# Five buffers for the gathers, ten for the chunks, later sums of sets, and a register load moved to its branch

## The chip, the cores and the metric

The kernel is one program on one core of a Trainium2 chip. The metric is the device time of one execution in microseconds (us). TensorE is called PE, VectorE DVE, ScalarE ACT, GpSimd POOL and SyncE SP, as in the profile.

## The reference, cut to what matters

Two transformer blocks follow each other on 256 tokens of width 1024 (float32). The first ends in a mixture of experts (32 experts, two for each token). The second ends in a layer that looks up a table of 16384 "keys", and the change is in that layer, apart from one register load in the experts. The layer computes:

```python
# per token: 8 heads, 16 of 16384 entries each, so 128 picked entries
eidx = jnp.take_along_axis(cidx, pos, axis=-1)
g = jax.nn.softmax(best, axis=-1)
a = jnp.einsum('chkd,cd->chk', u_tab[eidx], xc)      # u_tab, v_tab: 16384 x 1024
wgt = (jax.nn.gelu(a) * g)
return jnp.einsum('chk,chkd->cd', wgt, v_tab[eidx])
```

## The kernel before

The key layer treats its 256 tokens in two ways at the same time.

**160 tokens by the whole table (the chunks).** The table is read in 128 chunks of 128 entries. The U loop (128 chunks `ut`, line 1640) multiplies each chunk with the 160 tokens: eight matmuls 128x160 on PE give the products of 128 entries, ACT takes them through the gelu (L1601, L1604) into a tile `B`. From chunk `C0` = 40 on, 40 steps of `gbuild` put the routing weights into `B`, four tokens at a step: DVE and ACT prepare (L1949 to L1955), PE multiplies (L1965), DVE multiplies into `B` (L1968, whose shape holds the number of chunks that are done: 128x104x4 stands beside chunk 104). A step falls due every 2.2 chunks (88 chunks for 40 steps). The V loop (128 chunks `v`, line 1648) then multiplies `B` with the table V, and the eight PSUM banks `acc` collect all 128 chunks. A chunk is 512 KB. Chunks come in through the queue of SP (L87, and L76 for the slices of the tile `xm`), in turn into 14 buffers: four `wA`, three `hi`, three `lo` and four slices of `xm`. A load can start when PE has done with the buffer's chunk of 14 before.

**96 tokens by gathers.** They form three sets of 32 tokens. For a set, 32 gathers (L1765, POOL, an indirect DMA of 128 rows of U and V, 1 MB each) bring the rows that were picked, four entries of each token at a time. For each gather DVE takes the dot products with the tokens (L1793, into `ga`), ACT the gelu of 128 numbers (L1794), DVE multiplies with the weight (L1777) and adds the V half to the set's sum (L1779; L1784 for the first of a set). The sums are called `xa`, `xd0`, `xd1` (`xd` in the profile). When a set is complete, eight small matmuls (L1653, 128x32) add it to `acc`. These read the sum, and PE executes in order.

The order of the gathers is that of a generator, `gathered`: each `next` issues the dot of one gather, the add of the one before and a new fetch. The function `gathers` calls it 9 times in 20 chunks of the U loop and 7 times in 20 chunks of the V loop. A fetch also waits for the matmul of PE that was written last when it was written (`pace_pe`), so it can't run ahead of that place. Before, three fetches are written first, and then one behind each add, two gathers ahead of the dot:

```python
for i in range(3):
    fetch(i)
...
    if i:
        add(i - 1)
        fetch(i + 2)
```

The gathers' tiles `g` come from a pool of three (`gp`), in which some earlier tiles of the layer lie too. A scheduler puts the instructions of each engine into one order ahead of the run; it may move an instruction up or down where the data allow it, and the engine then executes in that order.

The set's sum is put in the V loop behind the first chunk from the third on at which the generator has completed the set:

```python
if c > 1 and ns < len(self.sums):
    for k in range(8):
        summed(ns, k)
    ns += 1
```

In the experts, `many` is the count of the fullest expert. All engines load it into a register (`nc.values_load`), and the branch `tc.If(many > 64)` in `overflow` (L924) reads it. Before, the load is written ahead of the loop over the experts.

Of the kernel before, what the change touches and what calls it, by code (L numbers as in the profile page):

```python
# [8 lines left out]
F32 = mybir.dt.float32  # L9
# [10 lines left out]
D = 1024  # L20
S = 256
# [23 lines left out]
class K:  # L45
# [693 lines left out]
    def moe(self):  # L739
        nc, me, A = self.nc, self.me, self.A  # L740
# [34 lines left out]
        def v(shape, dt=F32):  # L775
            return self.T(me, [128] + shape, dt)
# [56 lines left out]
        cnt, cmax, cmi = v([32]), v([1]), v([1], I32)  # L833
# [1 line left out]
        nc.vector.tensor_reduce(cmax, cnt, axis=AX.X, op=OP.max)  # L835
        nc.vector.tensor_copy(cmi, cmax)
        self.R, self.W, self.cnt, self.cmi, self.xnh, self.xnl = R, W, cnt, cmi, xh, xl
        many = nc.values_load(cmi[0:1, 0:1], min_val=0, max_val=S)
        wg = A["w_gate"].rearrange("e (p k) f -> e p k f", p=128)
        wu = A["w_up"].rearrange("e (p k) f -> e p k f", p=128)  # L840
        wd = A["w_down"].rearrange("e (p j) d -> e p j d", p=128)
# [62 lines left out]
        cur = experts(0, 28)  # L904
        for _ in bg:
            pass

        pools = self.wpools
        self.wi = 0
# [632 lines left out]
    def peer(self):  # L1542
        nc, A = self.nc, self.A
        tt, ts, stt = nc.vector.tensor_tensor, nc.vector.tensor_scalar, nc.vector.scalar_tensor_tensor
        xm = self.xm
# [42 lines left out]
            next(rg)  # L1588
        self.expand(x32)

        w4 = self.T(self.px, [128, 4, 1024], F32, "xm")
        self.wpools = [(self.wA, "wA")] * 4 + [(self.hp, "hi")] * 3 + [(self.hp, "lo")] * 3
        self.wpools += [(None, w4[:, i, :]) for i in range(4)]
        self.wi = 0
        gb = ga = self.pace_pe = None
        tau = 0
# [12 lines left out]
        def gathers(n):  # L1609

            nonlocal ga
            if ga is None:
                if not self.picked:
                    return
                ga = self.gathered()
                self.g0, self.gn = n, 0

            while self.gn < min(nj, (n - self.g0) * 9 // 20 if n < 128 else
                                (128 - self.g0) * 9 // 20 + (n - 128) * 7 // 20):
                next(ga, 0)  # L1620
                self.gn += 1
# [25 lines left out]
        def prod(c, k, w):  # L1647
            self.pace_pe = nc.tensor.matmul(acc[k][:, N0:], w[:, k * 128:(k + 1) * 128], B[:, c, :],  # L1648
                                            start=c == 0, stop=c == 127)

        def summed(s, k):

            nc.tensor.matmul(acc[k][:, s * self.GN:(s + 1) * self.GN], self.sums[s][:, k * 128:(k + 1) * 128], self.sel,  # L1653
                             start=False, stop=False)

        ns = 0
        for c in range(126):
            gathers(128 + c)
            w = self.wload(A["v"][c], [1024])
            for k in range(8):  # L1660
                prod(c, k, w)
            if c > 1 and ns < len(self.sums):
                for k in range(8):
                    summed(ns, k)
                ns += 1
# [89 lines left out]
    def gathered(self):  # L1755

        nc, A = self.nc, self.A
        stt = nc.vector.scalar_tensor_tensor
        J, n = self.GJ, self.NS * self.GJ
        buf, acc = {}, self.T(self.rt, [128, D], F32, "xa")  # L1760

        def fetch(i):
            if i < n:
                buf[i] = self.T(self.gp, [128, 2 * D], F32, "g")
                ins = nc.gpsimd.indirect_dma_start(  # L1765
                    out=buf[i], out_offset=None, in_=A["uv"],
                    in_offset=bass.IndirectOffsetOnAxis(ap=self.gi[:, i // J, i % J:i % J + 1], axis=0))
                if self.pace_pe:

                    self.tc.add_manual_dep(ins.ins, self.pace_pe.ins.name, mybir.DependencyInfo(  # L1770
                        mybir.DependencyClass.Sync, mybir.DependencyReason.DATA), reason="pace")

        def add(i):
            nonlocal acc
            s, j = i // J, i % J
            t, a, w = buf.pop(i)[:, D:], self.ga[:, s, j:j + 1], self.gw[:, s, j:j + 1]
            nc.vector.tensor_tensor(w, w, a, op=OP.mult)  # L1777
            if j:
                stt(acc, t, w, acc, op0=OP.mult, op1=OP.add)  # L1779
            else:  # L1780
                if s:

                    acc = self.gx[s - 1]
                nc.vector.tensor_scalar(acc, t, w, None, op0=OP.mult)  # L1784
            if j == J - 1:
                self.sums.append(acc)

        for i in range(3):
            fetch(i)
        for i in range(n):  # L1790
            s, j = i // J, i % J
            t, a = buf[i][:, 0:D], self.ga[:, s, j:j + 1]
            stt(t, t, 1.0, self.gx[s], op0=OP.mult, op1=OP.mult, accum_out=a)  # L1793
            nc.scalar.activation(a, a, AF.Gelu_apprx_tanh)  # L1794
            if i:
                add(i - 1)
                fetch(i + 2)
            yield
        add(n - 1)

# [354 lines left out]
```

## Time and profile before

| | us |
|---|---|
| median of 3 runs (1623.05 to 1627.79) | 1625.93 |
| the profiled execution | 1625.43 |
| its span in the trace | 1623.6 |
| PE busy in the span | 1527.8 |

The times of the trace count from the start of the span. The profiled execution took 1.8 us more than its span, and it lies 0.5 us under the median. The U loop begins on PE at about 982 us and the V loop at 1304.78 us; the last of its products ends at 1607.9 us, and what follows is the norm of the result and its way out.

### The profile page before, as it was taken

Reading aid. Unit: us, or ns where it says so; the run is one execution under the profiler, and the core shown is the slowest. Engines: PE = TensorE matmul, PEld = TensorE weight load, DVE = VectorE, ACT = ScalarE, POOL = GpSimd, SP = SyncE. Lnnn points to the kernel's source line nnn. Section 1 sums busy time; section 2 is a strip of 40 time slices with the busy share of each in tenths; the row PEclk is TensorE's granted clock in tenths of the full one; section 3 lists DMA queues with packets and bytes.
Section 4 is the critical chain, followed back from the end, with each engine's and each line's share of the span. In section 5 each row is a group of like instructions: output and inputs, shape, how many; then the busy total and the mean of one; then the engine's idle time right before and its main releaser. Section 6 shows DMA issues by size and latency. Waiting matters only on the chain. (4 is left out here: it accounts for less than half of the span.)

```text
span 1623.6 us, 25732 instructions
## 1 busy us (share of the span) xinstructions
PE 1527.8 (94%) x9872; PEld 1200.8 (74%) x9872; DVE 960.9 (59%) x2117; ACT 496.0 (31%) x1222; POOL 120.1 (7%) x122
## 2 busy tenths in 40 slices
PE   7999799999999997979999899999999999699996
PEld 6978644543444443358679699999999999699996
DVE  6986622344535432279888899856667656544443
ACT  4444332232222221155344543235444400000001
POOL 0000000000000000000000100311111112111111
PEclk9999899999999998989999999999999999799998
DMA  9548779999999998965657558999999999999992
GB/s 371 182 132 301 273 277 381 381 418 410 418 419 418 419 418 342 417 223 155 210 185 270 185 169 303 376 404 345 366 363 356 357 409 415 416 413 413 414 414 80
DMA packets 135324, 536.53 MB, mean 330 GB/s; under 512 B 16179, under 2 KB 17180, under 8 KB 122780
## 3 DMA queue, kind: packets, MB, share of 16 engines
q1 hardware_dynamic: 117184, 426.07, 69.1%
q0 software_dynamic: 13824, 100.67, 15.5%
q10 hardware_dynamic: 4188, 8.09, 1.4%
q8 instruction: 79, 1.29, 0.3%
q14 instruction: 49, 0.40, 0.1%
HBM read 532.57 MB, written 2.10 MB: 329 GB/s over the span
## 5 line engine op out<-in xcount | busy, mean ns | idle before, releaser
L1793 DVE SCALAR_TENSOR_TENSOR g<-g,xd 128x1024 f32<-128x1024 f32 x96 | 117.5, 1224 | 140.6 <-DMA g<-in_uv_dram,gi 140.6
L1031 PE MATMUL ps<-wB,XT 128*64 128x512 f32 x492 | 133.2, 609 | 4.7 <-PEq L924 4.6
L1765 POOL DMA_INDIRECT g<-in_uv_dram,gi x96 | 98.8, 1029 | 505.6 <-PE ps L1648 121.1
L132 PE MATMUL ps<-xh,hi 128*128 128x256 f32 x416 | 122.9, 296 | 1.6 <-ACT hi L97 1.6
L1067 DVE SCALAR_TENSOR_TENSOR eyl<-ps,slotw,eyh 64x512 fp32r<-64x512 f32 x64 | 47.6, 743 | 119.0 <-ACT eyh L1066 118.7
L138 PE MATMUL ps<-xh,lo 128*128 128x256 f32 x416 | 117.4, 283 | 0.5 <-DVE lo L98 0.5
L137 PE MATMUL ps<-xl,hi 128*128 128x256 f32 x416 | 117.5, 283 | 0.3 <-DVE xl L305 0.3
L1794 ACT ACTIVATE ga<-ga 128x1 f32<-128x1 f32 x96 | 19.4, 202 | 314.9 <-DVE g L1793 314.9
L1031 PEld LDWEIGHTS ps<-wB,XT 128*64 128x64 f32 x492 | 39.6, 139 | 80.5 <-issue 74.0
L97 ACT ACTIVATE hi<-wA 128x1024 fp32r<-128x1024 f32 x63 | 66.6, 1059 | 76.6 <-PE ps L137 28.8
L98 DVE TENSOR_TENSOR lo<-wA,hi 128x1024 fp32r<-128x1024 f32 x63 | 77.7, 1237 | 20.2 <-ACT hi L97 18.2
L1640 PE MATMUL ps<-x,wA 128*128 128x160 f32 x608 | 87.4, 302 | 0.1
L1648 PE MATMUL ps<-B,wA 128*128 128x160 f32 x608 | 85.9, 300 | 0.0
L1640 PEld LDWEIGHTS ps<-x,wA 128*128 128x128 f32 x608 | 84.9, 193 | 0.3 <-issue 0.3
L132 PEld LDWEIGHTS ps<-xh,hi 128*128 128x128 f32 x416 | 79.3, 191 | 7.7 <-issue 4.4
L1080 DVE TENSOR_TENSOR h<-h,ps 128x512 f32<-128x512 f32 x64 | 42.2, 682 | 70.3 <-PE ps L1078 70.3
L1648 PEld LDWEIGHTS ps<-B,wA 128*128 128x128 f32 x608 | 83.5, 190 | 0.0
L137 PEld LDWEIGHTS ps<-xl,hi 128*128 128x128 f32 x416 | 79.4, 191 | 3.9 <-issue 3.1
L1640 PE MATMUL ps<-x,xm 128*128 128x160 f32 x576 | 81.4, 299 | 0.0
L1648 PE MATMUL ps<-B,xm 128*128 128x160 f32 x576 | 81.2, 302 | 0.0
L1779 DVE SCALAR_TENSOR_TENSOR xd<-g,gw,xd 128x1024 f32<-128x1024 f32 x62 | 79.7, 1285 | 2.1
L1648 PEld LDWEIGHTS ps<-B,xm 128*128 128x128 f32 x576 | 80.1, 193 | 0.0
(531 smaller groups left out, 3364.4 us busy)
## 6 DMA issues: line engine op xcount, KB each, us to landing
wB<-in_w_gate_dram SPq DMA_DIRECT2D x70, 512.0 KB
wB<-in_w_down_dram SPq DMA_DIRECT2D x63, 512.0 KB
wB<-in_w_up_dram SPq DMA_DIRECT2D x53, 512.0 KB
wA<-in_ws_dram SPq DMA_DIRECT2D x51, 512.0 KB
wA<-in_ut_dram SPq DMA_DIRECT2D x38, 512.0 KB
wA<-in_v_dram SPq DMA_DIRECT2D x38, 512.0 KB
wA<-in_w_gate_dram SPq DMA_DIRECT2D x36, 512.0 KB
wA<-in_w_up_dram SPq DMA_DIRECT2D x36, 512.0 KB
```

The lines of the kernel that those rows point to most:

```text
L97: ins = self.nc.scalar.activation(hi, w, AF.Copy)
L98: self.last_split = self.nc.vector.tensor_tensor(lo, w, hi.bitcast(F32), op=OP.subtract)
L132: ins = mm(ps, ah, bh, start=first, stop=False)
L137: mm(ps, ah, bl, start=False, stop=False)
L138: mm(ps, al, bh, start=False, stop=last)
L1031: nc.tensor.matmul(p[64 * s:64 * s + 64, :], XT[:, k, :], w[s][:, a, :], start=k == 0, stop=k == 7)
L1067: nc.vector.scalar_tensor_tensor(y[1][r, s, :], p[r, :], w, y[0][r, s, :].bitcast(F32), op0=OP.mult, op1=OP.subtract)
L1640: self.pace_pe = nc.tensor.matmul(p, w[:, k, :], x32[:, k, N0:], start=k == 0, stop=k == 7)
L1648: self.pace_pe = nc.tensor.matmul(acc[k][:, N0:], w[:, k * 128:(k + 1) * 128], B[:, c, :], start=c == 0, stop=c == 127)
L1765: ins = nc.gpsimd.indirect_dma_start(out=buf[i], out_offset=None, in_=A["uv"], in_offset=bass.IndirectOffsetOnAxis(ap=self.gi[:, i // J, i ...
L1779: stt(acc, t, w, acc, op0=OP.mult, op1=OP.add)
L1793: stt(t, t, 1.0, self.gx[s], op0=OP.mult, op1=OP.mult, accum_out=a)
```

## The change

It gives the gathers two more buffers and takes four from the chunks: the tile `xm` holds two gathers now, so that there are five in all, and the chunks keep `wA`, `hi` and `lo`, ten in all. Five fetches are written first, and then each four gathers ahead of its dot. The sum of a set is written eight chunks later than its completion. The load of `many` is written behind the loop over the first 28 experts.

```diff
-        many = nc.values_load(cmi[0:1, 0:1], min_val=0, max_val=S)
...
         cur = experts(0, 28)
         for _ in bg:
             pass
+        many = nc.values_load(cmi[0:1, 0:1], min_val=0, max_val=S)
...
-        w4 = self.T(self.px, [128, 4, 1024], F32, "xm")
+        self.xg = self.T(self.px, [128, 2, 2 * D], F32, "xm")
         self.wpools = [(self.wA, "wA")] * 4 + [(self.hp, "hi")] * 3 + [(self.hp, "lo")] * 3
-        self.wpools += [(None, w4[:, i, :]) for i in range(4)]
...
-        ns = 0
+        ns, ready = 0, []
...
-            if c > 1 and ns < len(self.sums):
+            if len(ready) < len(self.sums):
+
+                ready.append(max(2, c + 8))
+            if ns < len(ready) and c >= ready[ns]:
                 for k in range(8):
                     summed(ns, k)
                 ns += 1
...
-                buf[i] = self.T(self.gp, [128, 2 * D], F32, "g")
+                buf[i] = self.xg[:, i % 5 - 3, :] if i % 5 > 2 else self.T(self.gp, [128, 2 * D], F32, "g")
...
-        for i in range(3):
+        for i in range(5):
             fetch(i)
...
-                fetch(i + 2)
+                fetch(i + 4)
```

Three places show what the scheduler makes of it. The first is PE in the V loop, at the sum of the second set (`xd_1993`): the last two products of one chunk and the first three of the sum's eight matmuls; the next chunk's products follow those. Before, 36 chunks of the V loop stand ahead of it:

```order
L1648 MATMUL ps_12620<-B_8958,lo_13044 128x160
L1648 MATMUL ps_12621<-B_8958,lo_13044 128x160
L1653 MATMUL ps_12614<-gsel_9975,xd_1993_9694 128x32
L1653 MATMUL ps_12615<-gsel_9975,xd_1993_9694 128x32
L1653 MATMUL ps_12616<-gsel_9975,xd_1993_9694 128x32
```

Now 44 chunks stand ahead of it:

```order
L1647 MATMUL ps_12638<-B_8958,wA_13162 128x160
L1647 MATMUL ps_12639<-B_8958,wA_13162 128x160
L1652 MATMUL ps_12632<-gsel_9975,xd_1993_9694 128x32
L1652 MATMUL ps_12633<-gsel_9975,xd_1993_9694 128x32
L1652 MATMUL ps_12634<-gsel_9975,xd_1993_9694 128x32
```

The eight matmuls moved behind eight more chunks. (The sum of the first set moved from behind 3 chunks to behind 9.)

The second place is DVE in the U loop, where the second set begins: its first add (L1784 before, L1786 now, gather 33 of 96) and the step of `gbuild` beside it. Before, it stands beside chunk 104:

```order
L1793 SCALAR_TENSOR_TENSOR g_11466,ga_9947<-g_11466,xd_1994_9695 128x1024
L1949 TENSOR_TENSOR x_2099_10558<-iotb_8959,lTi_9074 128x1024
L1777 TENSOR_TENSOR gw_9946<-gw_9946,ga_9947 128x1
L1605 TENSOR_TENSOR B_8958<-B_8958,qp_12035 128x116
L1784 TENSOR_SCALAR xd_1993_9694<-g_11466,gw_9946 128x1024
L1605 TENSOR_TENSOR B_8958<-B_8958,qp_12056 128x116
L1968 TENSOR_TENSOR B_8958<-B_8958,ps_12059 128x104x4
```

Now it stands beside chunk 88:

```order
L1795 SCALAR_TENSOR_TENSOR g_11380,ga_9947<-g_11380,xd_1994_9695 128x1024
L1951 TENSOR_TENSOR x_2105_10566<-iotb_8959,lTi_9074 128x1024
L1779 TENSOR_TENSOR gw_9946<-gw_9946,ga_9947 128x1
L1786 TENSOR_SCALAR xd_1993_9694<-g_11380,gw_9946 128x1024
L1604 TENSOR_TENSOR B_8958<-B_8958,qp_11680 128x88
L1604 TENSOR_TENSOR B_8958<-B_8958,qp_11700 128x88
L1970 TENSOR_TENSOR B_8958<-B_8958,ps_11703 128x88x4
```

The gathers' work moved up by 16 chunks here. Over the whole U loop, 42 dots stood ahead of the last step of `gbuild` on DVE, and 51 stand there now; ahead of the first step it was 9 and is 12.

The third place is POOL's queue at the first gathers. Before, they all go to `g`:

```order
L1765 DMA g_10058<-in_uv_dram,gi_9945 128x2048
L1765 DMA g_10060<-in_uv_dram,gi_9945 128x2048
L1765 DMA g_10062<-in_uv_dram,gi_9945 128x2048
L1765 DMA g_10113<-in_uv_dram,gi_9945 128x2048
L1765 DMA g_10163<-in_uv_dram,gi_9945 128x2048
```

Now the fourth and the fifth gather go to `xm`, and the scheduler put them ahead of the third (`g_10064`):

```order
L1767 DMA g_10060<-in_uv_dram,gi_9945 128x2048
L1767 DMA g_10062<-in_uv_dram,gi_9945 128x2048
L1767 DMA xm_9739<-in_uv_dram,gi_9945 128x2048 x2
L1767 DMA g_10064<-in_uv_dram,gi_9945 128x2048
L1767 DMA g_10119<-in_uv_dram,gi_9945 128x2048
```

Two things show nothing to move: the register load (TENSOR_LOAD) stands at the same row as before on each of the five engines, on PE between the last product of the first 28 experts and the branch; and up to the U loop all five engines have the same instructions in the same order. At the very end of PE's order the products of the last two chunks are now interleaved bank by bank, where before all eight of chunk 126 stood ahead of those of chunk 127.

## Rows read from the trace of the kernel before

**Rows 1.** The page: the chain that ended last, share of the span by line.

```profile
PE ps L1640 13%; PE ps L1648 12%; DMA g<-in_uv_dram,gi 5%; PE ps L1965 2%; DVE g L1793 1%; DVE xd L1779 1%; DVE B L1902 0%; DVE lo L98 0%; DMA gi<-g 0%; DMA wA<-in_wq_dram 0%; PE ps L137 0%; PE ps L138 0%; PE ps L132 0%; DVE g L1833 0%; DVE B L1904 0%
```

**Rows 2.** The chain in order of time: start us, us, what.

```profile
1083.20 0.89 PE ps L1965 x8
1084.09 4.35 PE ps L1640 x32
...
1404.29 199.22 PE ps L1648 x1456
```

**Rows 3.** Waits from 1304 to 1401 us: us in total, times, longest.

```profile
POOL g L1765 <- DVE xd L1779: 64.7, 18, 6.2
DVE g L1793 <- DMA g<-in_uv_dram,gi: 29.4, 20, 4.2
...
PE ps L1653 <- DVE xd L1779: 15.7, 1, 15.7
```

**Rows 4.** Timeline of PE: start us, us, [idle before and releaser].

```profile
1311.30 1.87 PE L1653 MATMUL ps<-gsel,xa 128*128 128x32 f32 x16
...
1378.29 6.68 PE L1648 MATMUL ps<-B,lo 128*128 128x160 f32 x48
1400.67 3.62 PE L1653 MATMUL ps<-gsel,xd 128*128 128x32 f32 x16 [15.70 <-DVE xd L1779]
1404.11 8.15 PE L1648 MATMUL ps<-B,xm 128*128 128x160 f32 x48
```

**Rows 5.** Windows: us, busy PE, PEld, DVE, ACT, POOL; granted clock, DMA share, GB/s.

```profile
1086.00:1195.00 109.00, 109.00 (x831) 109.00 (x831) 71.51 (x155) 50.56 (x206) 15.19 (x16) 1.00 0.96 362
...
1385.00:1401.00 16.00, 0.33 (x2) 0.33 (x2) 10.39 (x16) 0.81 (x4) 2.81 (x3) 0.65 1.02 414
...
1421.00:1500.00 79.00, 79.00 (x584) 79.00 (x583) 33.76 (x53) 2.63 (x13) 12.91 (x13) 1.00 1.02 413
```

**Rows 6.** DMA queues from 1304 to 1400 us (q0: gathers, q1: SP).

```profile
q0 software_dynamic: 2979, 21.70, 54.7%
q1 hardware_dynamic: 4946, 18.08, 46.9%
```

**Rows 7.** DMA issues from 1085 to 1304 us.

```profile
g<-in_uv_dram,gi POOLq DMA_INDIRECT x33
```

**Rows 8.** Waits of PE, whole span.

```profile
PE ps L1031 <- PEq L924: 4.6, 1, 4.6
```

**Rows 9.** Timeline of POOL at the first gathers.

```profile
1018.79 1.19 POOL L1765 DMA_INDIRECT g<-in_uv_dram,gi  x1 [38.02 <-DMA gi<-g]
...
1031.29 1.68 POOL L1765 DMA_INDIRECT g<-in_uv_dram,gi  x1 [10.07 <-DVE xa L1784]
...
1048.36 3.39 POOL L1765 DMA_INDIRECT g<-in_uv_dram,gi  x1 [10.36 <-DVE B L1907]
...
1106.61 0.94 POOL L1765 DMA_INDIRECT g<-in_uv_dram,gi  x1 [4.80 <-PE ps L1965]
```

**Rows 10.** Timeline of DVE at the first dots.

```profile
1025.98 1.23 DVE L1793 SCALAR_TENSOR_TENSOR g<-g,xd 128x1024 f32<-128x1024 f32 x1 [4.39 <-DMA g<-in_uv_dram,gi]
...
1040.27 1.23 DVE L1793 SCALAR_TENSOR_TENSOR g<-g,xd 128x1024 f32<-128x1024 f32 x1 [1.18 <-DMA g<-in_uv_dram,gi]
...
1051.70 0.23 DVE L1918 CAST x<-x 128x128 f32<-128x128 bf16 x1
```

**Rows 11.** Timeline of PE at the same place: a chunk, the transposes L1925, a chunk.

```profile
1047.12 2.34 PE L1640 MATMUL ps<-x,wA 128*128 128x160 f32 x16
...
1051.98 0.69 PE L1925 MATMUL ps<-ident,x 128*128 128x128 f32 x2 [2.41 <-DVE x L1918]
1052.46 3.77 PE L1640 MATMUL ps<-x,wA 128*128 128x160 f32 x16
```

**Rows 12.** Timeline at the end: the last product of PE, the last square of ACT.

```profile
1607.48 0.44 PE L1648 MATMUL ps<-B,wA 128*128 128x160 f32 x2
...
1612.18 0.42 ACT L1683 ACTIVATE g<-x 128x256 f32<-128x256 f32 x1
```

## Prediction

> **What bounds the kernel now.** I read the chain that ended last first. In the key layer it runs over the products of the U and V loops on PE, and in one stretch over something else: gathers take 5% of the span and DVE's work on them 2% [rows 1]. PE is busy throughout both loops except for this. The waits from 1304 to 1401 us name it: PE stands 15.70 us before the sum of the second set, because DVE has not finished its adds (L1779); in the same stretch DVE waits for gathers, 29.4 us, and POOL can't issue gathers because DVE has not freed their buffers, 64.7 us [rows 3]. So the second set is late, and its sum stands in PE's order ahead of work that is ready. From 1404.29 us the chain is PE alone for 199 us [rows 2].
>
> Why is it late? A step of `gbuild` falls due every 2.2 chunks, so the U loop takes 2.2 x 2.175 + 0.89 = 5.68 us a step [rows 2]; the generator asks for 9 gathers in 20 chunks, one each 5.74 us. From 1085 to 1304 us, 33 were issued [rows 7], one each 6.64 us: three buffers do not turn round faster when DVE looks at them at its own places. Where the sum stands tells the plan: behind chunk 35 of V, 65 calls, 53 of them in U. Only some 43 were done.
>
> The wait costs more than its length. Granted clock is 0.65 in the window around it [rows 5]: PE, idle, fell to its 1.2 GHz level. The sum took 3.62 us where the first set's took 1.87, and the three chunks behind it 8.15 where the three ahead of it took 6.68 [rows 4].
>
> **The change, part by part.** *The register load* stands at the same row of every engine's order as before: 0. What it could touch is PE's wait at the branch, 4.6 us [rows 8]; a gain of all of it, or as much again lost, are the ends, and neither has an instruction that moved. I take 0 and leave these ends out.
>
> *The sum, eight chunks later,* is due 8 x 2.175 = 17.4 us later [rows 2]; the wait is 15.70 us [rows 4]. This alone covers it, by 1.7 us only. The *five buffers* do more. On DVE 51 dots stand ahead of the last step of `gbuild` in place of 42, so at the V loop's start the gathers are 1 or 2 behind the plan in place of 10, and the second set is complete well ahead of its sum. Gained: 15.70 + (3.62 - 1.87) + (8.15 - 6.68) = **18.9 us** [rows 4].
>
> *What the gathers in U cost.* Nine more dots and adds at about 1.23 us each [rows 10] and small change are 24 us of DVE in some 220 us. DVE is busy 71.51 of 109 us there [rows 5], so 66% becomes 77%: covered by DVE's idle time, on an engine that PE does not wait for there (PE has 109.00 of 109.00). If that cover were gone, each `gbuild` step would be late by up to 0.6 us, 24 us in all; I take 0. The transfers: chunks need 0.524 MB in 5.68/2.2 = 2.58 us, 203 GB/s, gathers now 1.049 MB in 5.74 us, 183 GB/s; sum 386. It moved 362 there, and 413 to 414 where it is kept full [rows 5]. It fits. In V the demand is 241 for chunks (0.524/2.175) and 169 for gathers (7 in 20 chunks), 410 GB/s, as in the stretch from 1421 to 1500 us, where 413 moved and PE did not wait: covered, but with 1% to spare. That the gathers start V ahead, and not behind, is what keeps it so.
>
> *Ten buffers for chunks.* A load is asked for ten chunks ahead, 21.7 us in place of 30.4. Nothing is lost while a load takes less. The danger is a long row of gathers. In the catch-up from 1304 to 1400 us q0 moved 21.70 MB and q1 18.08 [rows 6]: while gathers queue, they come each 4.64 us and chunks get 188 GB/s. Ten chunks less two under way are 4.2 MB in hand. Such a row stands at the beginning. From about 1021 us [rows 9] to chunk 40 at some 1078 us [rows 2] PE needs 241 GB/s, 53 too many, and loses 57 x 0.053 = 3.0 MB. After that it needs 203; the row lasts until DVE's places, 5.7 us apart, have used it up: with 12 dots ahead of the first step and five buffers that is some 25 gathers, 116 us, and another 59 x 0.015 = 0.9 MB. Lost in all: 3.9 MB of 4.2. PE's own waits there (below) give back 1 MB. It holds, narrowly: I take 0; the other end is the second rival.
> The Trainium skill (DMA: Bandwidth & Descriptors, section Queues, rings and completion order) says that each DMA engine serves its queues in turn, packet by packet. By an even split of 414 chunks would get 207 GB/s, and the loss would be 57 x 0.034 = 1.9 MB: 0 with more to spare. The trace splits worse for the chunks, and I go by the trace.
>
> *The first gathers.* Before, DVE waits 4.39 us for gather 0 and 1.18 for another [rows 10], and PE waits 2.41 us at the transposes L1925 for the CAST that DVE issues at 1051.70; the chunk behind it takes 3.77 us, half clock, in place of 2.34 [rows 10, 11]. In DVE's new order five dots stand ahead of this CAST as before, but five adds in place of four; gathers 3 and 4 come right behind 0 and 1, about 4.6 us apart, which makes DVE wait about as long in sum as before. So the CAST comes about one add, 1.2 us, and some tenths later: **+1.5 us** on PE, which stands at the same place of its order. The ends: if all its wait goes, -2.41 - 1.43 = -3.8; if one gather more comes late by its whole spacing, +4.6 + 1.4 = +6. I take the value nearest to the rows of this place.
> POOL took 3.39 us for the issue at 1048.36 us, and 0.94 elsewhere [rows 9]. The Trainium skill (SBUF — State Buffer, section SBUF: two separate sides) says that DVE's two-port operations lock GpSimd out while it writes the descriptors of its own DMAs. By that rule this issue was held 2.45 us, and three gathers issued here would be 7.4 us late, inside DVE's wait for them: the end +6 would become +8.8 with the clock. The trace has one such issue; which operations are two-port ones it does not show.
>
> *The end.* Now each bank's last products stand together, so the first transposes can go out about two products earlier against the last product. ACT's squares end 4.7 us behind that product [rows 12], one of them each 0.54 us, and can begin two earlier: **-1.0 us**, between 0 and -1.2.
>
> The sum: -18.9 + 1.5 - 1.0 = -18.4 us; 1625.43 - 18.4 = 1607.0 for an execution like the profiled one, which lies 0.5 under the median of the three runs. I predict **1607 us**.
>
> **The rivals.**
> 1. *The wait moves to the beginning* (chance 0.08). Dots that now stand earlier in DVE's order than their gathers can land hold up the CAST, and PE at L1925. For it: PE waits there already, and gather 2 had to wait for a buffer 10.07 us [rows 9]. Against: the two `xm` buffers are free then. Time: +6 in place of +1.5, 1611.5.
> 2. *Chunks run dry* (0.15) between 1080 and 1140 us, if the first row of gathers costs 1 MB more than reckoned. PE then waits for single chunks, 1/0.241 = 4.2 us, and half a clock window of 1.4: 1612.6. For it: 0.3 MB in hand by the trace's split. Against: DMA reached only 362 GB/s on average behind this stretch, so what is lost is soon made good.
> 3. *The buffers of `xm` don't work as two* (0.04): the fourth gather holds the fifth, and the gathers begin V still 10 behind. Then chunks get 188 GB/s during the catch-up, 2.79 us each. The ten in hand last 25 chunks, 54 us, in which 54 x (1/4.64 - 1/6.2) = 3 gathers are made up; then PE takes 2.79 us a chunk and asks for a gather each 7.97 us, and the other 7 take 7/(1/4.64 - 1/7.97) = 78 us, 28 chunks at 0.62 us lost: 17 us, 1624, no change.
> 4. *Slower* (0.03): the gathers' queue never empties, and PE gets a chunk each 2.79 us. From 1140 to the V loop that loses 64 x 0.21 = 13 us, in V 0.62 us a chunk up to the last of 96 gathers at 1021 + 445 us, 58 chunks, 36 us: 1656. It decides where the row lasts to the ninth chunk of V. Against it, the pace lets no more than 53 + 4 gathers go in U, 264 us of the 284 up to V.
> 5. *Better than that* (0.02): the wait at L1925 goes, 1602 or less.
>
> The forecast has 0.68, its own range 1603 to 1611. **Numbers.** 0.3% is 4.9 us, about what a measurement of this kernel can tell from no change. Faster than 1621: forecast and rivals 1, 2 and 5, 0.93. Same: rival 3, 0.04. Slower: 0.03. The range from 1602 to 1613 takes in the forecast, rival 1 and most of rival 2; the rest lies beyond.
>
> **What would show it.** Right: no wait of PE for `xd`, the second sum at about 1.9 us, granted clock 1.00 from 1060 us to the end of V, V's 128 chunks and sums in 284 us instead of 303; dots just behind the plan at V's start, the gathers' rate 5.7 us in U, DMA there near 386 GB/s. Wrong: a wait of PE for a chunk's DMA (rivals 2 to 4), a wait longer than 4 us at the transposes (rival 1), or POOL waiting for DVE's adds for most of V (rival 3).

## The result and the profile after

The changed kernel takes 1605.41 us, median of 5 runs (1604.79 to 1606.51); the kernel before, run beside it, 1623.05 (1621.46 to 1627.79). The ratio is 0.9884, 95% interval 0.9867 to 0.9902: by the ratio 18.8 us or 1.2% faster, while the two medians lie 17.6 us apart. Forecast were 1607 us and a range of 1602 to 1613.

The profiled execution took 1605.19 us with a span of 1603.4, against 1625.43 and 1623.6. The starts of the first product of U and of V and the end of the last product of V in the two timelines divide the difference:

| us | before | after | difference |
|---|---|---|---|
| first product of U | 981.8 | 980.4 | -1.4 |
| U, to the first product of V | 323.0 | 324.0 | +1.0 |
| V, to the end of its last product | 303.1 | 284.5 | -18.6 |
| from there to the end of the span | 15.7 | 14.4 | -1.3 |

The first row is no effect of the change: ahead of the U loop all engines have the same order, and over the runs below U begins anywhere between 976 and 983 us. The +1.0 in U is within what executions of one order differ by (load_moved below has the order of before, and 326.4 us). What is left is in V, but for 1.3 us at the end.

PE's timeline of the kernel after, at the sums of the first and of the second set (start us, us, what):

```profile
1324.01 1.87 PE L1652 MATMUL ps<-gsel,xa 128*128 128x32 f32 x16
...
1401.86 1.87 PE L1652 MATMUL ps<-gsel,xd 128*128 128x32 f32 x16
1403.56 4.59 PE L1647 MATMUL ps<-B,wA 128*128 128x160 f32 x32
```

These answer to [rows 4]. Both sums now stand where the plan puts them, neither has an idle time in brackets, and both take 1.87 us; the second took 3.62. The two chunks behind it (32 matmuls) take 4.59 us, where before three (48) took 8.15. The windows say the same of the clock (columns as in [rows 5]):

```profile
1086.00:1195.00 109.00, 109.00 (x830) 108.77 (x829) 80.60 (x171) 51.74 (x209) 20.00 (x19) 1.00 1.02 414
...
1385.00:1401.00 16.00, 16.00 (x120) 16.00 (x119) 7.95 (x12) 0.61 (x3) 2.75 (x3) 1.00 1.03 416
```

In the window that held the wait PE is busy 16.00 of 16 us and the granted clock is 1.00 in place of 0.65. How far ahead the second set now is, DVE's timeline shows at its last add:

```profile
1361.48 1.28 DVE L1781 SCALAR_TENSOR_TENSOR xd<-xm,gw,xd 128x1024 f32<-128x1024 f32 x1
```

It ends at 1362.8 us, 39 us ahead of the sum. The waits from 1304 to 1401 us, to be read against [rows 3]:

```profile
POOL g L1767 <- PE ps L1647: 41.5, 8, 7.0
...
POOL xm L1767 <- PE ps L1647: 29.2, 6, 5.6
...
POOL g L1767 <- DVE xd L1781: 5.6, 1, 5.6
```

POOL waited 64.7 us for DVE's adds there, because the gathers were behind the plan. Now it waits for PE, which is the plan itself: a gather is issued when the chunk that it is tied to has been multiplied. Of the gathers' DMAs, 39 were issued between 1085 and 1304 us in place of the 33 of [rows 7], one each 5.62 us, 16 of them into the two `xm` buffers:

```profile
g<-in_uv_dram,gi POOLq DMA_INDIRECT x23
xm<-in_uv_dram,gi POOLq DMA_INDIRECT x16
```

What is left of PE's waits in U and V stands at the transposes of the second half of the routing (DVE's CAST first, then PE):

```profile
1049.88 0.22 DVE L1920 CAST x<-x 128x128 f32<-128x128 bf16 x1
```

```profile
1050.15 0.69 PE L1927 MATMUL ps<-ident,x 128*128 128x128 f32 x2 [3.62 <-DVE x L1920]
1050.63 4.47 PE L1639 MATMUL ps<-x,lo 128*128 128x160 f32 x16
```

The wait is 3.62 us where [rows 11] show 2.41, and the chunk behind it, at half clock, takes 4.47.

### The profile page after: what moved, and what is told of

The parts are those of the page before. It is cut to its first block, busy times and chain, and to the rows that moved or that the text cites. A ratio compares the mean times of both kernels' runs of the same rounds, so it can differ in the third digit from the quotient of the medians.

```text
span 1603.4 us, 25738 instructions
## 1 busy us (share of the span) xinstructions
PE 1525.1 (95%) x9872; PEld 1199.2 (75%) x9872; DVE 954.9 (60%) x2117; ACT 496.8 (31%) x1222; POOL 125.2 (8%) x122
## 5 line engine op out<-in xcount | busy, mean ns | idle before, releaser
L1795 DVE SCALAR_TENSOR_TENSOR g<-g,xd 128x1024 f32<-128x1024 f32 x58 | 70.9, 1223 | 83.0 <-DMA g<-in_uv_dram,gi 83.0
L1639 PE MATMUL ps<-x,wA 128*128 128x160 f32 x832 | 117.8, 300 | 0.0
L1639 PEld LDWEIGHTS ps<-x,wA 128*128 128x128 f32 x832 | 114.7, 191 | 0.0
L1647 PEld LDWEIGHTS ps<-B,wA 128*128 128x128 f32 x832 | 113.7, 190 | 0.0
L1639 PE MATMUL ps<-x,hi 128*128 128x160 f32 x624 | 88.5, 299 | 0.0
L1767 POOL DMA_INDIRECT g<-in_uv_dram,gi x58 | 65.0, 1121 | 293.7 <-PE ps L1647 115.3
L1647 PE MATMUL ps<-B,hi 128*128 128x160 f32 x608 | 86.6, 300 | 0.0
L1639 PE MATMUL ps<-x,lo 128*128 128x160 f32 x592 | 86.2, 304 | 0.0
L1639 PEld LDWEIGHTS ps<-x,hi 128*128 128x128 f32 x624 | 85.7, 190 | 0.2 <-issue 0.2
L1647 PE MATMUL ps<-B,lo 128*128 128x160 f32 x608 | 84.8, 299 | 0.0
```

Source lines behind the costliest of these rows:

```text
L1639: self.pace_pe = nc.tensor.matmul(p, w[:, k, :], x32[:, k, N0:], start=k == 0, stop=k == 7)
L1767: ins = nc.gpsimd.indirect_dma_start(out=buf[i], out_offset=None, in_=A["uv"], in_offset=bass.IndirectOffsetOnAxis(ap=self.gi[:, i // J, i ...
```

## The experiments

Each ratio is against the kernel before, run on the same chip in the same minutes; that kernel's own median was 1622.7 to 1625.5 us there. The loops' times are from one profiled execution each, taken as in the table above. Such an execution can lie off the median: sum_later's took 1618.29 us, v_eight's 1615.25, spread_six's 1604.73 and spread_mixed's 1598.70.

| kernel | median us | ratio, 95% interval | U us | V us |
|---|---|---|---|---|
| before (first profile) | 1625.93 | | 323.0 | 303.1 |
| after | 1605.41 | 0.9884 (0.9867, 0.9902) | 324.0 | 284.5 |
| sum_later | 1614.12 | 0.9928 (0.9915, 0.9942) | 323.7 | 295.2 |
| buffers_only | 1604.80 | 0.9875 (0.9860, 0.9889) | 324.4 | 284.5 |
| load_moved | 1623.71 | 1.0000 (0.9986, 1.0014) | 326.4 | 303.4 |
| ten_chunks | 1624.75 | 0.9995 (0.9976, 1.0015) | 324.2 | 302.7 |
| four_buffers | 1617.17 | 0.9966 (0.9951, 0.9980) | 320.7 | 297.1 |
| v_eight | 1613.07 | 0.9933 (0.9910, 0.9955) | 324.6 | 291.7 |
| seven_chunks | 1613.90 | 0.9942 (0.9922, 0.9962) | 331.3 | 284.7 |
| cast_first | 1607.88 | 0.9898 (0.9877, 0.9918) | 325.2 | 284.5 |
| spread_six | 1601.49 | 0.9857 (0.9840, 0.9874) | 322.4 | 287.1 |
| spread_seven | 1602.43 | 0.9869 (0.9850, 0.9887) | 323.5 | 284.6 |
| spread_mixed | 1601.16 | 0.9869 (0.9849, 0.9890) | 320.3 | 284.6 |
| after_again | 1606.18 | 0.9888 (0.9868, 0.9908) | 326.9 | 284.5 |

### The parts of the change alone

**sum_later**: the kernel before, with the sums eight chunks later.

```diff
-        ns = 0
+        ns, ready = 0, []
...
-            if c > 1 and ns < len(self.sums):
+            if len(ready) < len(self.sums):
+                ready.append(max(2, c + 8))
+            if ns < len(ready) and c >= ready[ns]:
```

Expected: 

> The kernel before with one part of the change: the sum of a set stands eight chunks later in V; three gather buffers and fourteen for chunks stay. Theory 1 (the place of the sum is what cost the time): the second set is complete at the same 1400.7 us and the sum is due at 1385 + 17.4 = 1402.4, so the 15.70 us and 3.22 us at half clock go and nothing takes their place: 1623.1 - 18.9 = 1604. Theory 2 (mine: late gathers keep a second price, the chunks): in the catch-up chunks get 188 GB/s where PE takes 241, and at V chunk 35 a chunk lands only 4 us ahead of its products. Without the stop PE runs on, the gathers are still about three behind, some 55 us of catch-up are left, and PE waits some 6 us for chunks: 1608 to 1612, with waits of PE for the DMAs of wA, hi, lo or xm between 1390 and 1450 us and none for xd.

Measured: 11.7 us faster (0.0072 of 1625.45), some three fifths of what the change brings. PE's waits from 1380 to 1430 us, and the second sum:

```profile
PE ps L1648 <- DMA wA<-in_v_dram: 2.7, 3, 1.3
PE ps L1648 <- DMA xm<-in_v_dram: 2.7, 4, 1.3
PE ps L1648 <- DMA lo<-in_v_dram: 1.3, 1, 1.3
PE ps L1648 <- DMA hi<-in_v_dram: 0.7, 1, 0.7
```

```profile
1408.32 2.44 PE L1648 MATMUL ps<-B,wA 128*128 128x160 f32 x16 [1.32 <-DMA wA<-in_v_dram]
1410.60 1.64 PE L1653 MATMUL ps<-gsel,xd 128*128 128x32 f32 x14
```

No wait for `xd` is left, and nine waits for chunks, 7.4 us, stand in its place. The gathers are as late as before; as long as they catch up, the DMA queues are full and the chunks come too slowly. So the wait for the sum had a second work, unseen: while PE stood, chunks were loaded. Theory 2 holds, and it had the loss somewhat too small: 1608 to 1612 us were expected, with some 6 us of waits.

**buffers_only**: the kernel after with the sum where it was.

```diff
-            if len(ready) < len(self.sums):
-                ready.append(max(2, c + 8))
-            if ns < len(ready) and c >= ready[ns]:
+            if c > 1 and ns < len(self.sums):
```

Expected: 

> The kernel after with the sum at its old place (behind chunks 2 and 35 of V); five gather buffers, ten for chunks. My theory: with five buffers the second set is complete at 1362.8 us, 22 us ahead of the old place of its sum at 1384.5, so the eight chunks are worth nothing beside the buffers: within 0.3% of 1605.4, no wait of PE for xd. Rival (the sum's place matters by itself, since adds and sums meet at the same time): a wait for xd of several us and 1610 or more.

Measured: 1604.80 us and V in 284.5, the same as with both parts. The second sum, in PE's timeline, and PE's waits in U and V:

```profile
1384.44 1.87 PE L1652 MATMUL ps<-gsel,xd 128*128 128x32 f32 x16
```

```profile
PE ps L1924 <- DVE x L1917: 5.9, 3, 3.9
PE ps L1639 <- DMA hi<-in_ut_dram: 1.1, 1, 1.1
```

The sum stands at its old place and waits for nothing. So the whole gain is the buffers'; beside them the eight chunks are worth nothing that can be measured. The last line is the forecast's second rival, in small: in this execution PE waited 1.1 us for chunk 45 of U.

**load_moved**: the register load at the branch, nothing else.

```diff
-        many = nc.values_load(cmi[0:1, 0:1], min_val=0, max_val=S)
...
         for _ in bg:
             pass
+        many = nc.values_load(cmi[0:1, 0:1], min_val=0, max_val=S)
```

Expected: 

> The kernel before with only the register load written at the branch. My theory: it stands at the same row on every engine, so nothing moves: within 0.3% of 1623.1, the wait at the branch 4.6 us as before. Rival (the load has a part in the gain): 2 to 5 us faster, with a shorter wait at the branch.

Measured: ratio 1.0000, and the waits of before:

```profile
PE ps L1653 <- DVE xd L1779: 13.8, 1, 13.8
PE ps L1925 <- DVE x L1918: 7.6, 2, 5.3
...
PE ps L1031 <- PEq L924: 5.0, 1, 5.0
```

The wait at the branch is there, 5.0 us. The middle line matters for another point: this kernel has the order of before on every engine, and yet its wait at the routing's transposes is 5.3 us where [rows 11] show 2.41. That wait differs by 3 us between executions of one order.

**ten_chunks**: the kernel before with the four `xm` buffers for chunks left unused.

```diff
-        self.wpools += [(None, w4[:, i, :]) for i in range(4)]
```

Expected: 

> The kernel before with ten buffers for chunks in place of fourteen, three for gathers, the sum at its old place. Theory 1 (ten are enough whatever the gathers do): no wait of PE for a chunk, 1623. Theory 2 (mine: ten are enough only where gathers are not behind): a chunk lands some 18 us ahead at V's start in place of 28, the catch-up takes 17 to 24 us of that by V chunk 35, so PE waits some 2 to 6 us for chunks there; but the second sum waits for the same gathers, and its wait of 15.7 us is shorter by as much: 1623 to 1626, with waits for chunk DMAs that the kernel before does not have. Theory 3 (they add up): 1629 or more.

Measured: 0.9995, no change, but PE's waits from 1304 to 1401 us are others than in [rows 3]:

```profile
PE ps L1647 <- DMA lo<-in_v_dram: 3.7, 3, 1.3
PE ps L1647 <- DMA hi<-in_v_dram: 3.1, 3, 1.3
PE ps L1647 <- DMA wA<-in_v_dram: 3.1, 4, 1.2
PE ps L1652 <- DVE xd L1778: 2.4, 1, 2.4
```

9.9 us for chunks and 2.4 for the sum, where it was 15.70 for the sum alone. Theory 2 holds in kind, its size (2 to 6 us) was too small. Both waits hang on the same late gathers, so one shortens by what the other takes.

### What sets the gathers' rate, and how much room the transfers have

**four_buffers**: the kernel after with one `xm` buffer in place of two.

```diff
-                buf[i] = self.xg[:, i % 5 - 3, :] if i % 5 > 2 else self.T(self.gp, [128, 2 * D], F32, "g")
+                buf[i] = self.xg[:, 0, :] if i % 4 == 3 else self.T(self.gp, [128, 2 * D], F32, "g")
...
-        for i in range(5):
+        for i in range(4):
             fetch(i)
...
-                fetch(i + 4)
+                fetch(i + 3)
```

Expected: 

> The kernel after with four gather buffers (one in xm) in place of five; ten for chunks, sums eight chunks later. DVE's order then has 44 dots ahead of the last step of the counting matrix, nearly as few as the 42 before, where five buffers give 51. My theory (the places of dots in DVE's order set the rate in U, not the number of buffers as such): gathers in U come each 6.5 us, they begin V some 7 behind, the catch-up takes the chunks' share, PE waits some 10 us for chunks and not for xd: 1613 to 1618. Rival (buffers set the rate, four take 6.64 x 3/4 = 5.0 us and so reach the plan): within 0.3% of 1605.4, no waits in V.

Measured: 1617.17 us; V takes 297.1. The issues between 1085 and 1304 us, PE's waits in V, and the windows 1336 to 1352 and 1352 to 1366:

```profile
g<-in_uv_dram,gi POOLq DMA_INDIRECT x25
xm<-in_uv_dram,gi POOLq DMA_INDIRECT x9
```

```profile
PE ps L1647 <- DMA lo<-in_v_dram: 4.6, 3, 2.0
PE ps L1647 <- DMA hi<-in_v_dram: 3.6, 3, 1.3
...
```

```profile
1336.00:1352.00 16.00, 11.07 (x75) 9.92 (x73) 11.73 (x17) 0.81 (x4) 3.75 (x4) 1.00 1.02 418
1352.00:1366.00 14.00, 9.41 (x53) 8.47 (x53) 9.80 (x16) 0.81 (x4) 4.17 (x3) 0.88 1.02 415
```

34 gathers, one each 6.4 us: nearly the 33 of three buffers. A buffer more is worth nothing here until the order on DVE uses it; the order with four has 44 dots ahead of the last step, that with five 51. My theory holds, and the traces say why: from 1085 to 1304 us DVE does not once wait for a gather's DMA, neither here nor in the kernel before. The gathers lay in their buffers until DVE's order came to them. Why the scheduler gives four so little, the runs don't show.

**v_eight**: the kernel after, eight gathers in 20 chunks of V.

```diff
-                                (128 - self.g0) * 9 // 20 + (n - 128) * 7 // 20):
+                                (128 - self.g0) * 9 // 20 + (n - 128) * 8 // 20):
```

Expected: 

> The kernel after with eight gathers in 20 chunks of V asked for in place of seven. My theory (DMA in V has 1% to spare): demand is 241 + 193 = 434 GB/s where 414 move, chunks lose 20 GB/s, the 8 to 9 us by which they land ahead at V's start are gone after some 100 us, and PE then waits some 8 us in sum until the last gather: about 1613, with waits for chunk DMAs from 1430 to 1540 us. Rival (DVE and the buffers hold the gathers back, or chunks are served first): within 0.3% of 1605.4 and no such wait.

Measured: 1613.07 us, and V takes 7.2 us longer. PE's waits from 1430 to 1560 us:

```profile
PE ps L1647 <- DMA hi<-in_v_dram: 1.8, 2, 1.3
PE ps L1647 <- DMA wA<-in_v_dram: 0.8, 3, 0.4
PE ps L1647 <- DMA lo<-in_v_dram: 0.5, 2, 0.2
```

Only 3.1 us are in brackets. The rest is in smaller pieces: from chunk 48 of V on, PE's gaps between chunks are 4.9 us longer in sum than in the kernel after, and the chunks themselves 1.2 us. So V has less to spare than the 24 GB/s that the eighth gather asks for. That it is as little as 1% this run does not show.

**seven_chunks**: the kernel after without the three `lo` buffers.

```diff
-        self.wpools = [(self.wA, "wA")] * 4 + [(self.hp, "hi")] * 3 + [(self.hp, "lo")] * 3
+        self.wpools = [(self.wA, "wA")] * 4 + [(self.hp, "hi")] * 3
```

Expected: 

> The kernel after with seven buffers for chunks in place of ten. My theory (ten are enough with little to spare: the least time by which a chunk lands ahead of its products was 4.7 us, at chunk 45 of U): three chunks fewer are 6.5 us less, so PE waits for chunks in the first row of gathers, some 2 us and what the clock costs, and 0 to 1 us at V's start, where it was 8.2 us: 1607 to 1612. Rival (the loads catch up by themselves, since a later load finds the queue as full): within 0.3% of 1605.4. Other rival (V too runs dry, since the gathers take 169 of 414 GB/s in rows): 1620 or more.

Measured: 1613.90 us (1611.62 to 1617.41), some 2 above what I expected; U takes 331.3 us, 7.3 more than in the kernel after, V 284.7. PE's waits from 1030 to 1100 us:

```profile
PE ps L1639 <- DMA wA<-in_ut_dram: 5.7, 5, 1.4
PE ps L1639 <- ACT ga L1796: 2.7, 2, 1.4
PE ps L1639 <- DMA hi<-in_ut_dram: 2.2, 2, 1.4
```

(The releaser ACT in the second line is one that had long been done: the wait is for several semaphores, and stands among the waits for chunks.) Three chunks fewer are 6.5 us less in hand, and of the 4.7 us that I counted on next to nothing was there (see the account of the ten buffers below). The first row of gathers is the one place where the number of chunk buffers decides; V, with three buffers fewer, does not notice.

### The wait at the transposes

**cast_first**: the kernel after, with dots 4 to 7 (counted from 0) and one add held behind the CAST, and no more than four gathers asked for before chunk 29. `after_cast`, whose text is left out here, makes an instruction depend on the CAST.

```diff
-            while self.gn < min(nj, (n - self.g0) * 9 // 20 if n < 128 else
+            while self.gn < min(nj, (4 if n < 29 else 99), (n - self.g0) * 9 // 20 if n < 128 else
...
-                stt(acc, t, w, acc, op0=OP.mult, op1=OP.add)
+                after_cast(stt(acc, t, w, acc, op0=OP.mult, op1=OP.add), i == 3)
...
-            stt(t, t, 1.0, self.gx[s], op0=OP.mult, op1=OP.mult, accum_out=a)
+            after_cast(stt(t, t, 1.0, self.gx[s], op0=OP.mult, op1=OP.mult, accum_out=a), 3 < i < 8)
...
-                nc.vector.tensor_copy(l[i], bf["e%d" % i])
+                self.cast = nc.vector.tensor_copy(l[i], bf["e%d" % i])
```

Expected: 

> The kernel after, with one more edit: the fourth to seventh dot and one add are written behind the CAST that the transposes of the second half of the routing wait for, so that one dot and no add stand between that half's last products and the CAST on DVE, where two dots and three adds stood. My theory (PE's 3.62 us and the chunks of 4.47 and 2.87 us behind it come from DVE's work on early gathers alone): the CAST comes at about 1045 in place of 1049.9, PE does not wait at those transposes, no chunk runs at half clock: 3.6 + 2.1 + 0.5 = 6.2 us less than 1605.4, 1599. Rival (the gathers of this place are then late and the row of gathers that follows takes the chunks' time): PE waits for chunks between 1080 and 1140 us and the time is within 0.3% of 1605.4.

Measured: 1607.88 us, no gain over after. PE's timeline there, with a part of its waits in U and V, and the DMA queues from 1066 to 1088 us (packets, MB, share):

```profile
1048.02 0.49 PE L1932 MATMUL ps<-ident,x 128*128 128x128 f32 x3
...
1072.00 2.41 PE L1639 MATMUL ps<-x,lo 128*128 128x160 f32 x16 [1.35 <-DMA lo<-in_ut_dram]
```

```profile
PE ps L1639 <- DMA wA<-in_ut_dram: 3.2, 3, 1.4
...
PE ps L1639 <- DMA lo<-in_ut_dram: 1.5, 2, 1.3
```

```profile
q0 software_dynamic: 836, 6.09, 66.8%
q1 hardware_dynamic: 837, 3.04, 34.6%
```

The wait and the half clock are gone, as I expected, and the rival is right all the same: the chunks run dry 20 us later, PE waits 5.8 us for them in sum, and that takes it back. PE's stop at the transposes was time in which chunks came in.

**spread_six, spread_seven, spread_mixed**: as cast_first, and the gathers asked for more evenly: fewer at first, more later. The requests of spread_six; spread_seven has `* 7 // 20, 12` and in V `50 + (n - 128) * 37 // 100`, and spread_mixed has the first half of spread_six and the second of spread_seven.

```diff
-            while self.gn < min(nj, (4 if n < 29 else 99), (n - self.g0) * 9 // 20 if n < 128 else
-                                (128 - self.g0) * 9 // 20 + (n - 128) * 7 // 20):
+            while self.gn < min(nj, 4 if n < 29 else min((n - self.g0) * 6 // 20, 10) + max(0, n - 44) * 10 // 20
+                                if n < 128 else 48 + (n - 128) * 39 // 100):
```

Expected of spread_six: 

> As cast_first (the CAST ahead of the fourth dot), and the gathers are asked for more slowly up to chunk 44 of U (6 in 20 chunks in place of 9, none between 44 and 46), then 10 in 20, and in V 39 in 100 chunks. My theory (what cast_first lost was the transfers' time: chunks 38 to 43 of U ran dry by 8 us, 1.9 MB, because the gathers go on in one row and PE no longer stands still for 6 us): some three gathers, 3.1 MB, less by 1085 us leave the chunks enough, PE waits neither at the transposes nor for chunks in U; U takes some 318 to 319 us in place of 325. Gathers begin V some 4 behind the plan of the kernel after, and 429 GB/s are asked for there where 414 move, so up to 4 us of waits for chunks late in V: 1599 to 1603. Rival (the transfers have nothing left to give over U and V together, 225 MB in 552 us from the first gather to the last chunk is 407 of 414 GB/s): what U gains V gives back, 1604 to 1608.

Expected of spread_seven: 

> As spread_six, milder: 7 in 20 chunks up to chunk 44 and 12 dots, then 10 in 20, and in V 37 in 100. My theory: about one gather, 1.05 MB, less by 1085 us than cast_first, so 8 us of waits for chunks in U become some 4; two dots more stand ahead of the last step of the counting matrix than in spread_six (50), and V asks for 419 GB/s: no waits there. 1601 to 1605. Rival (the row of gathers is set by DVE's order alone and holding back requests does nothing): 8 us of waits for chunks as in cast_first, about 1606.

Expected of spread_mixed: 

> The requests of spread_six in U (6 in 20 chunks up to chunk 44, then 10 in 20) with those of spread_seven in V (37 in 100). My theory (spread_six lost 2.5 us in V because 429 GB/s were asked for where 414 move; 419 is near enough): U as in spread_six, 322.4 us, and V as in the kernel after, 284.5, which is 1.6 us less than after in U and nothing more or less in V; with what varies ahead of U 1601 to 1604, 2 to 4 us under after_again on the same chip. Rival (the transfers are full over both loops, so gathers that U puts off must cost V the same): V 286 to 288 us, and no difference from after_again that can be measured.

Expected of after_again, the kernel after run beside spread_mixed: 

> The kernel after once more, on the chip of spread_mixed, so that the two stand side by side: within 0.3% of 1605.4 (ratio to the kernel before 0.987 to 0.990), 3 to 4 us of wait at the transposes of the second half of the routing, no wait in V.

Measured: 1601.49, 1602.43 and 1601.16 us, all three inside what I expected, and after_again 1606.18. Not all behind these times came as expected: in spread_six U takes 322.4 us, not 318 to 319, with 2.5 us of waits for chunks, and in after_again the wait at the transposes is 5.9 us, not 3 to 4. What spread_mixed and after_again have left of PE's waits in U and V:

```profile
PE ps L1932 <- DVE x L1925: 3.2, 2, 2.4
PE ps L1639 <- DMA lo<-in_ut_dram: 1.5, 2, 1.0
```

```profile
PE ps L1927 <- DVE x L1920: 9.0, 3, 5.9
```

From the start of chunk 40 to the end of U the three take 226.1 to 226.2 us, the two profiles of the kernel after 226.4 and 226.1, and cast_first 231.6: asked for more evenly, the gathers no longer make U lose behind chunk 40 what cast_first lost there. V is 284.6 us where 37 in 100 are asked for and 287.1 with 39. That the CAST's earlier place shortens U as a whole is not shown: U takes 320.3 to 323.5 us in the three and 324.0 and 326.9 in the kernel after, but 320.7 in four_buffers, where the CAST was not moved. Whether it makes a faster kernel the runs leave open: U and V together take 609.5, 608.1 and 604.9 us in the three, 608.5 and 611.4 in the kernel after, and on one chip the ratios are 0.9869 (0.9849 to 0.9890) and 0.9888 (0.9868 to 0.9908), whose intervals overlap.

## Why the prediction was right, step by step

**The wait and its clock**, forecast at -18.9 us: V is 18.6 us shorter. Right, and for the reason given: the sum came late because DVE's adds did, and the half clock behind the wait went with it. This is the one term of the sum that the runs can tell from nothing by far; U alone differs by 3 us between executions of one order.

**"This alone covers it, by 1.7 us only"**, of the sum eight chunks later: failed. sum_later shows the wait for `xd` gone and 7.4 us of waits for chunks in its place. I had compared the time at which the adds end with the time at which the sum is due, and left out that PE's stop was what kept the chunks in stock. The sum of the forecast was not touched, since the buffers do more than enough alone.

**The five buffers by way of DVE's order**: right, by buffers_only and four_buffers, and by DVE's waits in U, among which there is none for a gather. The second set is complete 39 us ahead of its sum, 22 ahead of the sum's old place.

**The register load, 0**: right, by load_moved.

**DVE in U**, forecast 77% busy: 80.60 of 109 us, 74%, and no wait of PE there.

**The transfers**, forecast 386 GB/s in U with 414 as the limit, and 1% to spare in V: the first window of U moved 414, since the chunk buffers that the row of gathers had emptied were being filled again. From 1085 to 1304 us it was 404. Right in what it says of PE, too low as a mean. In V, 24 GB/s more do not fit (v_eight); 19 more cost 2.5 us (spread_six, 429 asked for) and 9 more nothing (spread_seven and spread_mixed, 419). So the 1% was somewhat too narrow.

**Ten buffers for chunks, narrowly**: right in the result, by two errors that went against each other. I let the row of gathers go on to some 1140 us and gave the chunks 188 GB/s in it. From 1030 to 1090 us the queues of the kernel after moved (packets, MB, share):

```profile
q0 software_dynamic: 1982, 14.49, 58.5%
q1 hardware_dynamic: 2850, 10.39, 43.1%
```

That is 173 GB/s for the chunks, less than I had taken, but the row was over by about 1100 us: from gather 17 on (issued at 1091) a gather lies in its buffer 14 us before its dot. Even so, next to nothing was left over. By the semaphore updates in the trace the last part of chunk 45 landed 0.1 us ahead of its products, which began at 1090.9 us, and that of chunk 46 0.2 us ahead; at chunks 38 to 46 of cast_first, where PE did wait, it is 0.0 to 0.2 us too. In after_again 1.3 us were in hand at chunk 46. (The 4.7 us that the expectation of seven_chunks gives for chunk 45 are wrong: they go by when its number of bytes had come in, not by its last part.) That it came out so near, and still without a wait in the kernel after, is luck. In buffers_only and v_eight, whose U is that of after, the same place ran dry: from chunk 40 to the end of U they take 227.8 and 227.9 us; after takes 226.4, and before 226.1. So the second rival was nearer than its chance of 0.15 says, but its price is small: PE waits at most 1.4 us for a chunk there, in cast_first and seven_chunks too, and the granted clock stays at 1.00, where I had added 1.4 us for half clock.

**By an even split chunks would get 207 GB/s**: failed, and it was my reading of the rule, not the rule. See below.

**The first gathers**, forecast +1.5 us: not to be told apart. The wait was 2.4, 3.7, 5.3 and 5.2 us in before, sum_later, load_moved and ten_chunks, and 3.6, 3.9, 5.9 and 3.8 in after, buffers_only, after_again and v_eight: 4.15 and 4.3 in the mean. (In seven_chunks, where PE comes there later because it has waited for chunks, there is none.) The first rival (all of it moves here) is out. POOL's issues there took at most 1.68 us in the kernel after. The long issue of before was not chance: it took 3.39 us in all four profiles of the old order and came in none of the four of the new one, where 1.88 is the most. What held it no run shows.

**The end**, forecast -1.0 us: the last product and the last square of the kernel after are

```profile
1588.69 0.30 PE L1647 MATMUL ps<-B,hi 128*128 128x160 f32 x1
...
1592.09 0.42 ACT L1685 ACTIVATE g<-x 128x256 f32<-128x256 f32 x1
```

3.5 us from end to end where [rows 12] show 4.7: -1.2. Kernels with the old order at the end, load_moved and ten_chunks, still have 15.7 us from the last product to the end of the span; buffers_only, v_eight and seven_chunks, with the new one, have 14.4.

**The third and fourth rivals** are out: 16 of 39 gathers go into `xm`, two of five, and no wait of PE is left in V.

## What to carry to other kernels

A stop of the bounding engine is often also the time in which its stock is filled. Before a wait is taken away, by a later place of the one who waits (sum_later) or by work taken from its way (cast_first), reckon what the transfers must deliver once it is gone; removing the lateness itself, as the five buffers do, passed this reckoning here with nothing left over at chunk 45 of U.

Another buffer changes nothing until the order of the engine that frees it makes use of it: four gather buffers gave 34 gathers where three gave 33 and five 39. Count in the order before building on it, and look whether that engine ever waits for the buffer's DMA; here, in U, it did not.

## What the hardware showed that I had not expected

**Queues share by packets, not by bytes.** In the 22 us of cast_first in which both queues had work all the time, they moved 836 and 837 packets, one for one, and 6.09 and 3.04 MB: a gather's packets are twice as large (7.3 KB and 3.6 KB in the mean), so the chunks got 138 GB/s and the gathers 277. From 1064 to 1090 us of seven_chunks and from 1335 to 1360 us of four_buffers it is the same, 990 to 992 and 953 to 952. Where the gathers' queue runs empty now and then, the chunks get more: 173 in the first row of the kernel after, 188 in [rows 6]. The Trainium skill (DMA: Bandwidth & Descriptors, section Queues, rings and completion order) says that a DMA engine takes its queues in turn by packets, and the trace agrees: one for one. (A packet of the profile need not be a packet of that page; a gather and a chunk have 144 of the profile's each, so the ratio is the same.) I had read it as equal bytes.

**The length of a wait does not settle the clock.** In four_buffers PE stood 0.97 to 1.33 us ahead of every chunk from 1336 to 1352 us, was busy 11.07 of 16, and the granted clock was 1.00. After one wait of 1.96 us it fell:

```profile
1353.39 2.44 PE L1647 MATMUL ps<-B,lo 128*128 128x160 f32 x16 [1.32 <-DMA lo<-in_v_dram]
1357.79 3.35 PE L1647 MATMUL ps<-B,lo 128*128 128x160 f32 x16 [1.96 <-DMA lo<-in_v_dram]
```

The chunk behind it took 3.35 us, and the granted clock from 1352 to 1366 us was 0.88. Yet in the same execution a longer wait, 2.34 us at the transposes, left the clock at 1.00:

```profile
1049.47 0.44 PE L1927 MATMUL ps<-ident,x 128*128 128x128 f32 x2 [2.34 <-DVE x L1920]
1049.75 2.34 PE L1639 MATMUL ps<-x,lo 128*128 128x160 f32 x16
```

In the kernel before, 2.41 us at that place lowered it [rows 11]. So the short waits of 0.97 to 1.33 us cost little beyond their length here (2.44 us a chunk), and from which wait on the clock is lost as well, the runs don't settle.
